# A gated network's exact log decays: step-by-step sums predicted by TensorE prefix sums, one scan of 1.5 elements a step in place of two

## The chip, the cores and the metric

One core of one Trainium2 chip runs the whole program. The metric is the device time of one execution in microseconds; before the change three runs gave 4601.38, 4604.38 and 4605.38 us, median 4604.38.

## The reference

The program is one forward pass over 512 tokens of width 1024: block 1 (a mixer of sparse attention and a gated delta rule, then a mixture of experts) and two layers of block 2. The change lies in block 1's first norm and in the delta rule's log decays:

```python
g = -jnp.exp(a_log) * jax.nn.softplus(a_raw + dt_bias)     # a_raw: columns of h @ w_in, 8 heads
g_cum = jnp.cumsum(g, axis=-1)
decay = jnp.where(causal, jnp.exp(jnp.where(causal, g_cum[..., :, None] - g_cum[..., None, :], 0.0)), 0.0)
```

Here h is the normed input, scaled and shifted by the modulation `silu(c) @ ada_w + ada_b`. Exponentials of differences of sums that reach 1e7 make each rounding of the float32 sums count, so the kernel forms these few sums (16 x 128 columns of the modulation, 512 x 8 entries of a_raw, each of 1024 products) in the order in which the reference adds: one rounding per step.

## The kernel before, in words

The helpers record operations through an object; `mm` is a TensorE matmul, `act` a ScalarE activation, `tt`, `ts`, `stt` and `scan` are VectorE operations, `nc.gpsimd` is GpSimd. A tile framework orders each engine's operations ahead of time by their program order and readiness; on the chip each engine takes its own in that fixed order.

**Modulation (`exact_mod`, lines 737 to 824).** Weights are split into two parts of few bits (wh, wl), as is silu(c) (c1, c2, on diagonals dc), so that every product on TensorE is exact. A unit is 128 output columns (i = 2j + h) and half of the 1024 terms: 32 units. Its 512 leading products go to PSUM and are moved by ScalarE to xq, the middle ones to xms, the small ones to xz. VectorE then makes a first scan (the running sum, as it would be without the small parts), rounds it to the grid by adding and taking off a large M, GpSimd forms two differences, VectorE adds the middle ones, and a second scan of 1024 elements (two a step) rounds the true sum step by step. The second scan of a unit is recorded after the first operations of the next (`late`).

**Decays (`decay_chains`, lines 910 to 1018).** The same for the 512 x 8 entries: 32 units of (half of the terms, pair of heads, block of 128 tokens), eight chains in a row of 1040 elements, a scan of 1040 (az from aq and am), the rounding, the differences and a second scan of 2080 elements. It needs the modulation and each token's rstd. Then come `decay_sums`: a softplus in exact float32 pieces (a long chain of short VectorE operations) and sums over a chunk.

**What lies beside (`front`, drawn by `among` and `spend`, lines 318 to 334).** Each VectorE operation of the exact part adds 0.7 x (0.2 + elements / 960) to a debt, and while the debt is positive the next step of the front is recorded there. The front's steps have costs: keys and values of the memory 2 x 40, small gates 5, compression 32, keys, values, queries and compressed branch 54, attention 8 x 2 x 6.6 = 105.6; together about 277. What is left over is recorded at the end. The front's products use the weight slabs wraw, whi, wlo: 512 KB loaded on SP's queue, split by ScalarE and by VectorE or GpSimd in turn.

Of the eight PSUM banks, two (x) take the exact products, three (g) the gemms, two (t) small products, one (o) outputs.

Of the kernel before, what the change touches and what calls it, by code (L numbers as in the profile page):

```python
# [32 lines left out]
KT = 8  # L33
# [7 lines left out]
# float32 coefficients: exponential, logarithm, log1p (numerator, denominator)  # L41
# [11 lines left out]
# ---------------------------------------------------------------- host layout  # L53
# [41 lines left out]

def _dn_constants():
# [32 lines left out]
def _pack_pv(inp):  # L129
# [13 lines left out]
    add("n1g", _cols(inp["norm1_g"]))  # L143
    add("n2g", _cols(inp["norm2_g"]))
# [19 lines left out]
def pack(inp):  # L164
# [6 lines left out]
    a["ada_w"] = np.ascontiguousarray(inp["ada_w"][0].reshape(KT, 128, 24, 256).transpose(2, 1, 0, 3))  # L171
    w = inp["w_in"][0]
# [5 lines left out]
    a["w1_a"] = _kpn(av)  # L178
# [75 lines left out]
# ---------------------------------------------------------------- the program  # L254
class Net:
# [30 lines left out]
    # ---- small helpers  # L286
# [30 lines left out]
    # the steps of other, a generator of rough costs, among what VectorE does for main  # L317
# [41 lines left out]
    def sub(self, lo, src, hi):  # L359
        """src - hi in SBUF; of every lo_of, lo_pool on GpSimd"""  # L360
# [4 lines left out]
    # ---- weights and products  # L365
# [18 lines left out]
    def rsqrt(self, T, src, n, N=S, out=None):  # L384
        """(src / n + eps) ** -0.5: exponential of the logarithm, then a Newton step"""
# [13 lines left out]
    def sigmoid(self, T, src, shape, tag, bufs=1):  # L399
        """exp(-ln(1 + exp(-z)))"""  # L400
# [7 lines left out]
    def rms64(self, T, out, src, gcol, s, N=S, n=64, op_scale=None):  # L408
        """out = src * g * rsqrt(sum over each half of the partitions / n + eps)"""
# [7 lines left out]
    # ---- column sums of squares over features -> rstd broadcast over partitions  # L417
# [40 lines left out]
    def ada(self, T):  # L458
        """the modulation but for the first shift and scale"""
# [22 lines left out]
    def adaln(self, T, keep):  # L482
        """h = x * rstd * gain + shift"""
# [29 lines left out]
    def near_hi(self, T, a, hi, lo, tag, bits=12):  # L513
        """a rounded to 12 bits, and the rest"""
# [7 lines left out]
    def xprod(self, T, a, b, n):  # L522
        """minus a product, and the product's rounding error"""
# [9 lines left out]
    def xadd(self, T, out, m, e, c, n, big=False):  # L533
        """c - m + e in one rounding; c a tile, a number, or one number for each of equal parts; big: never smaller than m"""
# [3 lines left out]
        def take(o, x, rev=False):  # L538
            """c - x, or x - c"""
# [24 lines left out]
    def xfma(self, T, out, a, b, c, n, big=False):  # L564
        """a * b + c in one rounding"""
# [13 lines left out]
    def xhorner(self, T, y, x, xs, cs, n, big=True):  # L579
        """Horner's rule, each step in one rounding; the first two coefficients on the scalar engine"""  # L580
# [4 lines left out]
    def xexp(self, T, x, n):  # L585
        """exp as (y, 2 ** k)"""
# [15 lines left out]
        # minus the sum of the two parts, and its error  # L602
# [14 lines left out]
    def xdiv(self, T, out, a, b, n):  # L617
        """a / b, rounded once; a a tile or one"""
# [28 lines left out]
    def consts(self, T, rows, n):  # L647
        """[128, steps, parts] of numbers"""
# [6 lines left out]
    def xsoftplus(self, T, out, x, n):  # L655
# [8 lines left out]
        def same(x, k, i):  # L664
            """x, k times, and its parts"""
# [14 lines left out]
        # log1p by a rational function: denominator and numerator  # L680
# [14 lines left out]
        # log(1 + e), 1 <= 1 + e <= 2  # L695
# [22 lines left out]
        # the first below the threshold, the second above  # L718
# [8 lines left out]
    def grid(self, T, out, q, n):  # L727
        """a power of two between 4 and 8 times the largest entry of each row"""
# [8 lines left out]
    def exact_mod(self, X):  # L737
        """the shift and the scale of the first norm: one accumulator per column, one rounding per term"""
        nc = self.nc
        self.mod1 = X.tile([128, 16], F32, name="mod1")  # L740
        with self.pool("xm", side="right") as T:
# [9 lines left out]
            M = T.tile([128, 1], F32, name="xM")  # L751
            st2 = T.tile([128, 2, 2], F32, name="xst")
            def slab(j, half):
                w = T.tile([128, 4, 256], F32, name="xw", bufs=2)
                nc.sync.dma_start(w, self.I["ada_w"][j][:, 4 * half:4 * half + 4, :])
# [3 lines left out]
                self.tt(wl, w, wh, OP.subtract)  # L759
                return wh, wl  # L760

            def products(j, half, h):
                if h == 0:
                    self.xw = slab(j, half)
                wh, wl = self.xw
                cs = slice(128 * h, 128 * h + 128)
                q = T.tile([128, S], F32, name="xq", bufs=2)
                m = T.tile([128, S], F32, name="xms", bufs=2)
                z1 = T.tile([128, 512, 2], F32, name="xz1", bufs=3)
                for out, scale, terms in ((q, 1.0, ((wh, 0),)), (m, 1.0, ((wh, 1), (wl, 0))), (z1[:, :, 0], -1.0, ((wl, 1),))):  # L770
                    p = self.ps("x")
                    for kk in range(4):
                        for n, (a, i) in enumerate(terms):
                            self.mm(p[:, 128 * kk:128 * kk + 128], a[:, kk, cs], dc[:, i, 4 * half + kk, :],
                                    kk == 0 and n == 0, kk == 3 and n == len(terms) - 1)
                    self.act(out, p, scale=scale)
                return q, m, z1

            def sums(j, half, h, q, m, z1):
                st = st2[:, h]  # L780
                z0 = T.tile([128, 513, 2], F32, name="xz0", bufs=2)
                if j == 0 and h == 0 and half == 0:
                    self.grid(T, M, q, "m")
                gh = z0[:, :, 1]
                if half == 0:
                    nc.gpsimd.memset(gh[:, 0:1], 0.0)
                    g0 = d0 = 0.0
                else:
                    g0, d0 = st[:, 0:1], st[:, 1:2]
                    self.act(gh[:, 0:1], g0)  # L790
                self.scan(gh[:, 1:], q, m, g0, op0=OP.add, op1=OP.add)
                self.ts(gh[:, 1:], gh[:, 1:], M, M, OP.add, OP.subtract)
                self.act(z1[:, :, 1], gh[:, 1:])
                t = z0[:, 1:, 0]
                nc.gpsimd.tensor_tensor(t, gh[:, 1:], gh[:, :512], op=OP.subtract)
                nc.gpsimd.tensor_tensor(t, q, t, op=OP.subtract)
                self.tt(t, t, m, OP.add)

                def rest():
                    i = 2 * j + h  # L800
                    d = z1.rearrange("p a b -> p (a b)")
                    self.scan(d, z0[:, 1:].rearrange("p a b -> p (a b)"), d, d0, op0=OP.add, op1=OP.subtract)
                    if half == 0:
                        self.act(st[:, 0:1], gh[:, 512:513])
                        self.act(st[:, 1:2], d[:, 1023:1024])
                    else:
                        self.tt(self.mod1[:, i:i + 1], gh[:, 512:513], d[:, 1023:1024], OP.add)
# [3 lines left out]
            units = [(j, half, h) for j in range(8) for half in range(2) for h in range(2)]  # L811
            ready = products(*units[0])
            late = None
            for n, u in enumerate(units):
                now = ready
                if n < 31:
                    ready = products(*units[n + 1])
                f = sums(*u, *now)
                if late is not None:
                    late()  # L820
                late = f
            late()
            self.tt(self.mod1, self.mod1, self.pv("ada_b", 0, 16), OP.add)
# [1889 lines left out]
```

## Time and profile before

| | |
|---|---|
| median of 3 runs | 4604.38 us (4601.38 to 4605.38) |
| profiled execution, its span | 4600.1 us, 53904 instructions |
| mean granted TensorE clock | 0.900 of full speed |
| PE busy | 3975.4 us (86%) |
| DVE busy | 3086.1 us (67%) |
| ACT busy | 2088.8 us (45%) |
| POOL busy | 1763.2 us (38%) |

PE is TensorE's matmuls, PEld its weight loads, DVE VectorE, ACT ScalarE, POOL GpSimd, SP the queue that issues most loads. All times are in us from the start of the span unless a column says ns. Matmuls are pipelined: the duration of one holds a tail in which the next already runs, so that a busy PE need not be a full one. The granted clock has two levels, 1.0 (2.4 GHz) and 0.5 (1.2 GHz); a mean lies between.

### The profile page before, as it was taken

The numbers are of one execution on the slowest core, as the hardware profiler recorded it, in microseconds if no ns is written. First come the engines' busy times: TensorE is split into PE (matmuls) and PEld (weight loads), VectorE is DVE, ScalarE is ACT, GpSimd is POOL, SyncE is SP. The second block draws the span as 40 slices with busy tenths as digits, with TensorE's granted clock in tenths as the row PEclk, the third lists the DMA queues.
The fourth block names the chain that finished last, engine by engine and source line by source line (L and its number), as shares of the span: only waits on it lengthen the run. The fifth ranks groups of instructions, "written<-read, shape, count | busy, mean of one in ns | idle before, by whom it ended". The sixth has DMA issues, their size and how long they took to land. (4 is left out here: it accounts for less than half of the span.)

```text
span 4600.1 us, 53904 instructions
## 1 busy us (share of the span) xinstructions
PE 3975.4 (86%) x19368; PEld 3192.1 (69%) x19368; DVE 3086.1 (67%) x5074; ACT 2088.8 (45%) x3514; POOL 1763.2 (38%) x1084
## 2 busy tenths in 40 slices
PE   5667757777897888979989999999999898999998
PEld 3566545555776676767867777788877676787886
DVE  8988999998865587857657565433378566665542
ACT  3444546554223276833436544443244365544432
POOL 3445544632321335223326442232234354423431
PEclk9678867777887899989999999999999999999999
DMA  4233201113311588931222242222211132332222
GB/s 141 83 109 111 64 21 46 32 37 118 92 56 36 194 311 318 358 114 57 73 64 88 78 135 83 92 96 91 92 60 64 57 102 66 118 120 74 92 93 82
DMA packets 178958, 473.62 MB, mean 103 GB/s; under 512 B 17176, under 2 KB 32600, under 8 KB 178304
## 3 DMA queue, kind: packets, MB, share of 16 engines
q1 hardware_dynamic: 171872, 445.99, 29.3%
q0 software_dynamic: 6816, 24.15, 1.5%
q8 instruction: 154, 2.52, 0.2%
q14 instruction: 116, 0.95, 0.1%
HBM read 429.66 MB, written 38.29 MB: 102 GB/s over the span
## 5 line engine op out<-in xcount | busy, mean ns | idle before, releaser
L363 POOL TENSOR_TENSOR wlo<-wraw,whi 128x1024 fp32r<-128x1024 f32 (+4 forms) x244 | 566.1, 2320 | 1106.2 <-ACT whi L315 1041.9
L303 PE MATMUL ps_g<-ha,whi 128*128 128x512 f32 x2184 | 896.6, 411 | 63.0 <-DVE mraw L343 22.8
L315 ACT ACTIVATE whi<-wraw 128x1024 fp32r<-128x1024 f32 (+4 forms) x489 | 481.3, 985 | 948.8 <-PE ps_g L303 734.8
L303 PE MATMUL ps_g<-ha,wlo 128*128 128x512 f32 x2184 | 891.5, 408 | 6.3 <-DVE wlo L363 4.2
L303 PE MATMUL ps_g<-hl,whi 128*128 128x512 f32 x2184 | 892.3, 409 | 0.0
L303 PEld LDWEIGHTS ps_g<-ha,whi 128*128 128x128 f32 x2184 | 424.6, 194 | 177.8 <-DVE mraw L343 22.0
L303 PEld LDWEIGHTS ps_g<-ha,wlo 128*128 128x128 f32 x2184 | 424.3, 194 | 108.9 <-DVE wlo L363 4.9
L303 PEld LDWEIGHTS ps_g<-hl,whi 128*128 128x128 f32 x2184 | 424.6, 194 | 102.1 <-issue 3.5
L363 DVE TENSOR_TENSOR wlo<-wraw,whi 128x1024 fp32r<-128x1024 f32 (+4 forms) x245 | 308.5, 1259 | 187.7 <-ACT whi L315 182.2
L339 DVE TENSOR_TENSOR_SCAN az<-az,az 128x2080 f32<-128x2080 f32 x32 | 153.3, 4792 | 4.4 <-POOL az L993 4.2
L303 PE MATMUL ps_g<-fal,whi 128*128 128x512 f32 x352 | 137.0, 389 | 0.0
L303 PE MATMUL ps_g<-fah,whi 128*128 128x512 f32 x352 | 137.0, 389 | 0.0
L303 PE MATMUL ps_g<-fah,wlo 128*128 128x512 f32 x352 | 136.9, 389 | 0.0
L353 DVE SCALAR_TENSOR_TENSOR h_R<-h_R,h_gd,ps_s 128x64 f32<-128x64 f32 x448 | 124.6, 278 | 11.9
L2314 POOL TENSOR_SCALAR mP<-mP,sfst 128x512 f32<-128x512 f32 x64 | 103.0, 1616 | 52.1 <-DVE sfst L2313 25.4
L303 PE MATMUL ps_g<-mlo,xh 128*128 128x512 f32 x272 | 111.8, 411 | 11.4 <-POOL mlo L1913 11.4
L303 PE MATMUL ps_x<-xdc,xwh 128*128 128x128 f32 x256 | 66.7, 350 | 63.1 <-ACT xdc L315 40.6
L1501 POOL TENSOR_TENSOR dnl<-dnn,dnc 128x512 f32<-128x512 f32 x48 | 68.5, 1439 | 137.1 <-DVE dnn L343 70.0
L2528 POOL TENSOR_SCALAR g2z<-g2z 128x512 f32<-128x512 f32 x48 | 81.8, 1705 | 99.8 <-DVE g2z L343 88.8
L988 POOL TENSOR_TENSOR az<-az 128x1024 f32<-128x1024 f32 x32 | 78.7, 2460 | 104.0 <-DVE az L349 69.3
L303 PE MATMUL ps_x<-adw,ahh 128*128 128x256 f32 x256 | 84.1, 392 | 37.8 <-ACT az L315 19.2
L343 DVE TENSOR_TENSOR x<-ps_g,x 128x512 f32<-128x512 f32 x48 | 33.0, 691 | 124.8 <-PE ps_g L303 124.8
(996 smaller groups left out, 10446.2 us busy)
## 6 DMA issues: line engine op xcount, KB each, us to landing
wraw<-w_fm SPq DMA_DIRECT2D x169, 512.0 KB, 3.5
wraw<-f_w SPq DMA_DIRECT2D x120, 512.0 KB, 3.4
mrawa<-moe_g SPq DMA_DIRECT2D x18, 1024.0 KB, 10.6
mrawb<-moe_d SPq DMA_DIRECT2D x18, 1024.0 KB, 6.7
adaw<-ada_w SPq DMA_DIRECT2D x64, 256.0 KB, 2.7
mrawa<-moe_u SPq DMA_DIRECT2D x16, 1024.0 KB, 9.2
mrawb<-moe_u SPq DMA_DIRECT2D x16, 1024.0 KB, 10.4
mrawb<-moe_g SPq DMA_DIRECT2D x14, 1024.0 KB, 10.7
```

The source lines that it names most:

```text
L303: self.nc.tensor.matmul(out, a, b, start=start, stop=stop)
L315: return self.nc.scalar.activation(out, in_, f, **kw)
L339: return self.nc.vector.tensor_tensor_scan(out, *args, **kw)
L343: return self.nc.vector.tensor_tensor(out, a, b, op=op)
L353: return self.nc.vector.scalar_tensor_tensor(out, a, s, b, op0=op0, op1=op1)
L363: e.tensor_tensor(lo, src, hi, op=OP.subtract)
L988: nc.gpsimd.tensor_tensor(t, gh[:, :, 2:], gh[:, :, 1:129], op=OP.subtract)
L1501: nc.gpsimd.tensor_tensor(nl, n_, dnc[:, 1 + lv, None, :].to_broadcast([128, 4, 128]), op=OP.mult)
L2314: nc.gpsimd.tensor_scalar(P, P, st[:, 3:4], None, op0=OP.mult)
L2528: self.nc.gpsimd.tensor_scalar(z, z, ZMIN, None, op0=OP.max)
```

## The change

The first scan, the rounding and the differences' first part are replaced. TensorE multiplies the weights with triangle tables (a prefix sum of the leading and middle products, `tri` scaled by c in `upto`, or by the weights in `times`) and adds M by one more product (`dm` with ones), so that the predicted running sum stands on the grid when it is in PSUM. ScalarE moves it out twice, as the sum and as its negative, into every third element of a row; GpSimd forms the difference d of neighbours; TensorE adds d (by a float32 product with the identity) to all the products and ScalarE moves the sum to the remaining third. One scan with in-row steps of two runs over 1.5 elements a step. The terms are reordered on the host (`_steps`), so that the reference's four accumulators are rows of their own: the modulation goes over all columns of the first half, then the second; the decays have four parts c of two k tiles, 64 units of two heads with both rows of 256 steps in one row of 774 elements. The split wl goes from VectorE to GpSimd, the slab xw has one buffer in place of two. The debt of the front grows by 2.0 with each unit besides what the scan adds, where VectorE's other operations had added theirs.

The parts of the diff that do work on the chip:

```diff
-    def spend(self, out):
+    def spend(self, out, more=0.0):
         if self.other is not None:
-            self.debt += self.ratio * (0.2 + math.prod(out.shape[1:]) / 960)
+            self.debt += more or self.ratio * (0.2 + math.prod(out.shape[1:]) / 960)
...
+            def upto(half):
+                tc = T.tile([128, 2, 1280], F32R, name="xtc")
+                at = 0
+                for kk in range(4):
+                    n = 512 - 128 * kk
+                    for i, c in enumerate((c1, c2)):
+                        self.act(tc[:, i, at:at + n], self.tri[:, :n], scale=c[:, 4 * half + kk:4 * half + kk + 1])
+                    at += n
+                return tc
...
             def slab(j, half):
-                w = T.tile([128, 4, 256], F32, name="xw", bufs=2)
-                nc.sync.dma_start(w, self.I["ada_w"][j][:, 4 * half:4 * half + 4, :])
+                w = T.tile([128, 4, 256], F32, name="xw")
+                nc.sync.dma_start(w, self.I["ada_x"][j][:, 4 * half:4 * half + 4, :])
...
-                self.tt(wl, w, wh, OP.subtract)
+                nc.gpsimd.tensor_tensor(wl, w, wh, op=OP.subtract)
...
+            def path(half, j, h):
...
+                a = T.tile([128, 1538], F32, name="xa", bufs=3)
+                p = self.ps("x")
+                at = 0
+                for kk in range(4):
+                    n = 512 - 128 * kk
+                    for m, (w, e) in enumerate(((wh, 0), (wh, 1), (wl, 0))):
+                        self.mm(p[:, 512 - n:], w[:, kk, cs], tc[:, e, at:at + n], kk == 0 and m == 0, False)
+                    at += n
+                self.mm(p, dm, self.onew, False, True)
...
+                self.act(a[:, 3::3], p, AF.Identity, bias=up)
+                self.act(a[:, 4::3], p, AF.Identity, scale=-1.0, bias=down)
+                d = T.tile([128, S], F32, name="xd", bufs=2)
+                nc.gpsimd.tensor_tensor(d, a[:, 0:1536:3], a[:, 4::3], op=OP.add)
 
                 def rest():
...
+                    p = self.ps("x")
+                    self.mm(p, self.ident, d, True, False)
+                    for kk in range(4):
+                        for n, (w, e) in enumerate(((wh, 0), (wh, 1), (wl, 0), (wl, 1))):
+                            self.mm(p[:, 128 * kk:128 * kk + 128], w[:, kk, cs], dc[:, e, 4 * half + kk, :], False, kk == n == 3)
+                    self.act(a[:, 2::3], p)
+                    self.scan(a[:, 3::2], a[:, 2::2], a[:, 3::2], st[:, i, 1:2] if half else 0.0, op0=OP.add, op1=OP.add)
...
+                    self.spend(None, self.step)
...
+            late = []
+            for u in [(half, j, h) for half in range(2) for j in range(8) for h in range(2)]:
+                late.append(path(*u))
+                if len(late) > 1:
+                    late.pop(0)()
...
+        for c in range(4):
...
             for pr in range(4):
...
+                def times(out, m, e):
+                    n = m.shape[1]
+                    for i in range(2):
+                        nc.gpsimd.tensor_tensor(out[:, i], m[:, None, :].to_broadcast([128, 2, n]),
+                                                wp[:, i, 2 * c + e, hs, None].to_broadcast([128, 2, n]), op=OP.mult)
+
+                times(t0, self.tri[:, :256], 0)
+                times(t1, self.tri[:, :128], 1)
+                for e in range(2):
+                    times(dg[:, e], self.ident, e)
...
+                    for n, (h, i) in enumerate(((hh, 0), (hh, 1), (hl, 0))):
+                        self.mm(p, h[:, 0, tk], t0[:, i].rearrange("p h i -> p (h i)"), n == 0, False)
+                        self.mm(p3[:, :, 128:], h[:, 1, tk], t1[:, i], False, False)
+                    self.mm(p, dm[:, b], self.onew, False, True)
+                    self.act(t[:, :, 7::3], p3, AF.Identity, bias=M[:, b, 1:2])
+                    self.act(t[:, :, 8::3], p3, AF.Identity, scale=-1.0, bias=M[:, b, 0:1])
+                    d = T.tile([128, 2, 256], F32, name="ad", bufs=2)
+                    nc.gpsimd.tensor_tensor(d, t[:, :, 4:772:3], t[:, :, 8::3], op=OP.add)
...
+                        p = self.ps("x")
+                        self.mm(p, self.ident, d.rearrange("p h i -> p (h i)"), True, False)
+                        for e in range(2):
+                            diag(p, tk, e, ((hh, 0), (hh, 1), (hl, 0), (hl, 1)), False, e == 1)
+                        self.act(t[:, :, 6::3], p.rearrange("p (h i) -> p h i", h=2))
+                        f = t.rearrange("p h i -> p (h i)")
+                        self.scan(f[:, 1::2], f[:, 0::2], f[:, 1::2], 0.0, op0=OP.add, op1=OP.add)
+                        nc.gpsimd.tensor_tensor(st[:, c, b, 2 * pr:2 * pr + 2], t[:, :, 772], t[:, :, 773], op=OP.add)
+                        self.spend(None, self.step)
...
+            self.step = 2.0
```

## Rows read from the trace of the kernel before

**Rows 1.** The page's 40 slices: DVE's busy tenths, 115 us each.
```profile
DVE  8988999998865587857657565433378566665542
```
**Rows 2.** Stretches: length, busy us (instructions) of PE, PEld, DVE, ACT, POOL; clock; DMA.
```profile
39.00:1064.00 1025.00, 719.08 (x3302) 570.03 (x3302) 926.20 (x1333) 515.30 (x1061) 497.30 (x328) 0.75 0.22 71
...
996.00:1064.00 68.00, 52.92 (x171) 35.38 (x169) 60.51 (x312) 34.22 (x85) 9.05 (x11) 0.70 0.34 103
...
500.00:550.00 50.00, 44.36 (x224) 37.09 (x225) 41.97 (x26) 25.33 (x48) 31.06 (x19) 0.90 0.23 74
600.00:650.00 50.00, 26.86 (x110) 22.14 (x110) 46.28 (x48) 20.04 (x37) 21.70 (x18) 0.53 0.04 11
1300.00:1350.00 50.00, 44.78 (x348) 37.52 (x346) 40.11 (x91) 15.45 (x29) 15.53 (x11) 0.71 0.14 43
```
**Rows 3.** The stage by tile: az, xz (DVE, ACT, POOL); xwl, ps_x (PE first).
```profile
39.00:1064.00 1025.00, 300.38 (x112) 83.94 (x144) 244.10 (x164) 0.75 0.22 71
39.00:1064.00 1025.00, 180.31 (x144) 47.98 (x112) 117.79 (x78) 0.75 0.22 71
39.00:1064.00 1025.00, 67.89 (x256) 57.08 (x256) 20.91 (x14) 0.75 0.22 71
39.00:1064.00 1025.00, 224.78 (x1024) 187.67 (x1024) 166.04 (x288) 0.75 0.22 71
```
**Rows 4.** DVE groups of the stage, scans: count | busy us, mean ns | idle before, releasers.
```profile
L339 DVE TENSOR_TENSOR_SCAN az<-az,az 128x2080 f32<-128x2080 f32 x32 | 153.3, 4792 | 4.4 <-POOL az L993 4.2
L339 DVE TENSOR_TENSOR_SCAN az<-aq,am 128x1040 f32<-128x1040 f32 x32 | 87.3, 2727 | 5.3 <-ACT am L315 5.0 <-issue 0.3
...
L339 DVE TENSOR_TENSOR_SCAN xz<-xq,xms 128x512 f32<-128x512 f32 x16 | 19.5, 1216 | 11.2 <-ACT xms L315 10.9
```
**Rows 5.** ACT groups of the stage, same columns.
```profile
L315 ACT ACTIVATE az<-ps_x 128x512 f32<-128x512 f32 x64 | 40.5, 634 | 24.6 <-DVE az L339 18.1 <-DVE smst L1124 4.2 <-DVE smst L348 1.4
L315 ACT ACTIVATE aq<-ps_x 128x512 f32<-128x512 f32 x64 | 37.9, 592 | 13.2 <-PE ps_x L303 10.7 <-POOL az L954 1.4 <-POOL wlo L363 0.4
L315 ACT ACTIVATE az<-az 128x1040 f32<-128x1040 f32 x32 | 37.7, 1178 | 24.5 <-DVE az L349 20.5 <-DVE smst L343 2.5 <-DVE smst L348 1.2
...
L315 ACT ACTIVATE xz<-xz 128x512 f32<-128x512 f32 x32 | 21.9, 684 | 60.5 <-DVE xz L349 60.3
...
L315 ACT ACTIVATE rsv<-ps_t,ce 128x512 f32<-128x512 f32 x6 | 4.1, 684 | 1.9 <-DVE rst L343 1.9
```
**Rows 6.** POOL groups of the stage, same columns.
```profile
L363 POOL TENSOR_TENSOR wlo<-wraw,whi 128x1024 fp32r<-128x1024 f32 x33 | 93.1, 2820 | 80.4 <-ACT whi L315 80.4
...
L795 POOL TENSOR_TENSOR xz<-xz 128x512 f32<-128x512 f32 x32 | 55.5, 1733 | 129.9 <-DVE xz L349 114.7 <-DVE mod L343 11.9 <-DVE cact L343 3.2
...
L946 POOL TENSOR_TENSOR adw<-apid,aw 128x1024 fp32r<-128x1024 f32 x16 | 37.1, 2335 | 3.4 <-DVE aw L353 2.7 <-DVE aw L343 0.5 <-PE ps_x L303 0.2
```
**Rows 7.** PE groups of the stage: the front's matmuls of 512 and 256 columns.
```profile
L303 PE MATMUL ps_g<-hl,whi 128*128 128x512 f32 x200 | 87.9, 440 | 0.0
...
L303 PE MATMUL ps_g<-whi,meml 128*128 128x256 f32 x128 | 37.8, 296 | 0.0
```
**Rows 8.** PE in order of time: start us, us, instruction; 128, 256 and 512 columns.
```profile
89.33 0.27 PE L303 MATMUL ps_x<-xdc,xwh 128*128 128x128 f32 x1
89.44 0.27 PE L303 MATMUL ps_x<-xdc,xwl 128*128 128x128 f32 x1
...
104.55 7.07 PE L303 MATMUL ps_g<-fmw,cact 128*1 128x256 f32 x32
...
202.91 0.28 PE L303 MATMUL ps_g<-memh,whi 128*128 128x256 f32 x1
203.03 0.28 PE L303 MATMUL ps_g<-meml,whi 128*128 128x256 f32 x1
...
3000.07 0.39 PE L303 MATMUL ps_g<-ha,whi 128*128 128x512 f32 x1
3000.30 0.39 PE L303 MATMUL ps_g<-hl,whi 128*128 128x512 f32 x1
```

More of the change, by code (lines that the diff above doesn't have):

```diff
@@ L143, in _pack_pv @@
     add("n1g", _cols(inp["norm1_g"]))
+    add("n1gx", _cols(_steps(inp["norm1_g"][0])))
+    add("ada_bx", np.concatenate([_cols(_steps(inp["ada_b"][0, i * D:(i + 1) * D])) for i in range(2)], 1))
     add("n2g", _cols(inp["norm2_g"]))
@@ L171, in pack @@
     a["ada_w"] = np.ascontiguousarray(inp["ada_w"][0].reshape(KT, 128, 24, 256).transpose(2, 1, 0, 3))
+    ax = inp["ada_w"][0][:, :2 * D].T.reshape(2, D, D)
+    ax = np.concatenate([_steps(ax[i]) for i in range(2)]).T
+    a["ada_x"] = np.ascontiguousarray(ax.reshape(KT, 128, 8, 256).transpose(2, 1, 0, 3))
+    p = np.arange(128)
+    a["tri"] = np.concatenate([p[:, None] <= p[None, :], np.ones((128, 384), bool)], 1).astype(np.float32)
     w = inp["w_in"][0]
@@ L766, in products @@
                 cs = slice(128 * h, 128 * h + 128)
[L767 to L770, printed above, removed]
+                if half == i == 0:
                     p = self.ps("x")
                     for kk in range(4):
[L773 to L784, printed above, removed]
+                        self.mm(p[:, 128 * kk:128 * kk + 128], wh[:, kk, cs], dc[:, 0, kk, :], kk == 0, kk == 3)
+                    self.grid(T, M[:, 0:1], p, "m")
+                    self.ts(M[:, 1:2], M[:, 0:1], -1.0)
@@ L785, in sums @@
+                up, down = M[:, 1:2], M[:, 0:1]
                 if half == 0:
[L786 to L794 removed]
@@ L809, in sums @@
-                return rest
[L811 to L823, printed above, removed]
+                    nc.gpsimd.memset(a[:, 0:1], 0.0)
+                else:
+                    self.act(a[:, 0:1], st[:, i, 0:1])
+                    ud = T.tile([128, 2], F32, name="xud", bufs=3)
+                    self.act(ud[:, 0:1], st[:, i, 0:1], AF.Identity, bias=up)
+                    self.act(ud[:, 1:2], st[:, i, 0:1], AF.Identity, scale=-1.0, bias=down)
+                    up, down = ud[:, 0:1], ud[:, 1:2]
@@ L934, in decay_chains @@
-        for half in range(2):
-            hh = T.tile([128, 4, S], F32R, name="ahh", bufs=1)
-            hl = T.tile([128, 4, S], F32R, name="ahl", bufs=1)
-            for kk in range(4):
-                k = 4 * half + kk
-                t = (qs, ms)[kk % 2][kk // 2][:, 0:4, 2:]
-                nc.sync.dma_start(t, self.I["xT"][:, k, :].rearrange("p (c i) -> p c i", c=4))
+        wp = T.tile([128, 2, 8, 8], F32, name="awp")
+        self.near_hi(T, w, wp[:, 0], wp[:, 1], "aw")
+        M = T.tile([128, 4, 2], F32, name="aM")
@@ new lines, in decay_chains @@
+        dm = T.tile([128, 4, 128], F32R, name="adm")
+        st = T.tile([128, 4, 4, 8], F32, name="ast")
+        tiles = [T.tile([128, 2, 774], F32, name="aa%d" % i) for i in range(3)]
+        for t in tiles:
+            nc.gpsimd.memset(t[:, :, 0:6], 0.0)
+            for at, v in ((1, FAR), (2, -FAR)):
+                nc.gpsimd.memset(t[:, :, at:at + 1], v)
+        unit = 0
+        late = []
+        for c in range(4):
+            hh = T.tile([128, 2, S], F32R, name="ahh", bufs=2)
+            hl = T.tile([128, 2, S], F32R, name="ahl", bufs=2)
+            for e in range(2):
+                k = 2 * c + e
+                t = T.tile([128, 4, 128], F32, name="axs", bufs=2)
+                nc.sync.dma_start(t, self.I["xs"][:, k, :].rearrange("p (c i) -> p c i", c=4))
@@ L995, in rest @@
-                    def rest(z0=z0, z1=z1, gh=gh, s=s, half=half):
-                        d = z1.rearrange("p c a b -> p (c a b)")
-                        self.scan(d, z0.rearrange("p c a b -> p (c a b)"), d, 0.0, op0=OP.add, op1=OP.subtract)
-                        if half == 0:
-                            self.act(s[:, 0], gh[:, :, 129])
-                            self.act(s[:, 1], z1[:, :, 129, 1])
-                        else:
-                            nc.gpsimd.tensor_tensor(s[:, 0], gh[:, :, 129], z1[:, :, 129, 1], op=OP.add)
+                    if c == pr == 0:
+                        p = self.ps("x")
+                        for e in range(2):
+                            diag(p, tk, e, ((hh, 0),), e == 0, e == 1)
+                        self.grid(T, M[:, b, 0:1], p, "a")
+                        self.ts(M[:, b, 1:2], M[:, b, 0:1], -1.0)
+                        self.act(dm[:, b], self.ident, scale=M[:, b, 0:1])
@@ L1635, in exact @@
     def exact(self, X):
-        self.exact_mod(X)
-        self.exact_decay(X)
+        nc = self.nc
+        self.mod1 = X.tile([128, 16], F32, name="mod1")
+        self.gct = X.tile([128, 32], F32, name="gct")
+        with self.pool("xk", side="right") as K:
+            self.tri = K.tile([128, S], F32, name="tri")
+            nc.sync.dma_start(self.tri, self.I["tri"])
+            self.onew = K.tile([128, S], F32R, name="onew")
+            self.act(self.onew.rearrange("p (a b) -> p a b", a=4), self.ones[:, None, :].to_broadcast([128, 4, 128]))
+            self.step = 2.0
+            self.exact_mod(K)
+            self.exact_decay(K)
     def front(self, M):
```

119 lines of the change are left out of this document (35 added, 84 removed).

## The prediction

> **What bounds the kernel now.** I read the page's slices first: VectorE (DVE) stands at 8 or 9 tenths through the first eleven slices, some 1260 us, and nowhere after [rows 1]. The code changed runs there, beside the front (keys of the memory, gates, attention), so I next asked for the busy times of the stage from the first product on ps_x (39 us) to the end of the softplus (1064 us): 1025 us, DVE 926 of it (90%), TensorE (PE) 719, ScalarE (ACT) 515, GpSimd (POOL) 497 [rows 2]. The tile sums then say whose work that is: instructions on az, xz and xwl hold DVE for 300 + 180 + 21 = 501 us [rows 3]. So DVE's order of work sets this stage, and over half of it is what the change touches. What follows 1064 us isn't touched and should only move earlier.
>
> **The change, engine by engine.** It keeps the emission order (the front's steps are drawn by a debt), so I sum the work of each engine in the stage, old and new, and then ask what length such loads can pack into.
>
> *DVE.* The 501 us go: both scans, the rounding to the grid, the added products and the split of xw. What comes is 96 scans (32 of 768, 64 of 774 elements). The trace has scans of 512, 1040 and 2080 elements at 1.22, 2.73 and 4.79 us [rows 4]; per element that is 2.3 to 2.6 ns, so a scan of 770 lies between 1.77 and 2.02 us. I take 1.95, as these scans too will share the SBUF with POOL: 187 us. DVE: 926 - 501 + 187 = 612 us. It stops being the bound, by 314 us.
>
> *ACT.* It moves out per new unit three times 512 columns of PSUM, with a step of three elements on the write side. With a step of two it costs 0.63, contiguous 0.59, with a bias column 0.68 [rows 5]. I take 0.66: 96 x 3 x 0.66 = 190 us, and about 25 for tables, diagonals and carried columns. Going: 64 x (0.63 + 2 x 0.59) + 32 x 1.18 of the decay part, 32 x (0.63 + 2 x 0.59 + 0.68) of the other, about 25 of small ones: 258 us. ACT: 515 - 258 + 215 = 472. Were a step of three to cost half as much again, 567; still not the bound.
>
> *POOL.* Going: 244 + 118 us on az and xz [rows 3] and 37 on adw [rows 6]. Coming: 96 sums d of 512 elements, 16 splits of 1024, 16 sets of tables (2560 elements each). A sum of 512 read with a step of two took 1.73, a split 2.82, a table of 1024 elements 2.34 [rows 6]: 96 x 1.73 + 16 x 2.82 + 16 x 5.85 = 305, and some 25 for small ones. POOL: 497 - 399 + 330 = 428.
>
> The new sum d reads both inputs with a step of three floats (12 bytes); no row of before shows such a step on POOL. From the rows, its bounds are 1.17 us (half a table of 1024 elements) and 2.82 us (a whole split of 1024): -54 to +105 us on POOL against 1.73, which I take as the nearest row in size and step.
>
> The Trainium skill (GPSIMD Reference, section 7, Performance pitfalls for Q7 kernels) says that POOL reading SBUF with a step of more than 8 bytes pays about half as much again per element. By that rule d would cost 1.5 x 1.73 = 2.6 us, and POOL would stand at 511 in place of 428. No run shown here has that step.
>
> *PE.* Here the change puts its load. A matmul's duration counts a tail in which the next already runs, so I price by the distance of starts in dense runs at full clock: 128 columns 0.11 us, 256 0.12, 512 0.23, so 384 about 0.18; a plain float32 one of 256 columns 0.22 (32 in 7.07), so one of 512 about 0.44 [rows 8].
> - Before: 512 products of 128 and 512 of 256 columns on ps_x: 56 + 61 = 118 us.
> - A new unit of the modulation: prefix sums 3 x (0.23 + 0.18 + 0.12 + 0.11) = 1.9, the grid's diagonal 0.23, the float32 identity on d 0.44, 16 diagonal products 1.8: 4.35 us, x 32 = 139.
> - A new unit of the decays: 3 x (0.23 + 0.12) + 0.23 + 0.44 + 8 x 0.12 = 2.7 us, x 64 = 170.
> - The rest, unchanged: 600 matmuls of 512 columns (three groups like that shown), 768 of 256 (six groups) [rows 7], 128 of the first fast modulation at 0.22, and some 780 others between 0.11 and 0.23, taken at 0.15: 138 + 92 + 28 + 117 = 375.
> So PE goes from 493 to 684 us at full clock, +191. What this is in time hangs on the granted clock. In stretches of 50 us it was 0.90 where PE was busy for 44 of 50 us, 0.53 where 27, and once 0.71 at 45 [rows 2]. I take 0.90: 760 us. PE becomes the fullest engine.
>
> *How it packs.* PE 760, DVE 612, ACT 472, POOL 428. The chain of a decay unit (prefix on PE 1.3, two moves on ACT 1.3, d on POOL 1.7, products on PE 1.4, a move on ACT 0.7, scan on DVE 1.95) is some 8 us, but the next unit's prefix lies between d's start and the products. With one bank of ps_x for the prefixes and one for the products, a unit alone needs PE's own time and some 0.7 us of waits: 32 x 5.05 + 64 x 3.4 = 379 us, so the chain isn't the limit while front work fills the gaps. Two things are late next. The first is that engines of like load wait for each other in their fixed orders: I give PE's 760 us a tenth, 76. The second is the softplus, a chain of short DVE operations: it took 68 us with the last of the front beside it [rows 2]. The debt now grows by 2.0 and 0.7 x (0.2 + 770 / 960) = 0.7 a unit, 2.7; with the small operations (some 37) the modulation brings it to about 124, so the front's 277 cost units are used up after some 56 of the 64 decay units, and the chain runs uncovered; PE had 53 busy us there. I charge 44. Stage: 760 + 76 + 44 = 880 us in place of 1025, that is -145.
>
> A check from the other side: now 719 + 926 + 515 + 497 = 2657 busy us in 1025, 2.59 engines at once. With the new loads (PE in the same measure 719 - 225 [rows 3] + 309 / 0.9 = 837) it is 2349, at 2.59 again 907 us: -118. I stay with -145, because the fixed DVE order is no longer in the way.
>
> The loads added before the stage are small: two tables of 256 KB on SP's queue (512 KB loads land in under 5 us) and the slab xw with one buffer in place of two, which is reloaded once in two units (near 10 us): nothing.
>
> **Sum.** The profiled execution spans 4600.1 us, 4.3 below the median of the runs, 4604.4. 4600.1 - 145 + 4.3 = 4459, rounded to 4460.
>
> **Rivals.**
> 1. *TensorE stays at the clock it has* (the other side). The mean granted clock of the stage is 0.75 [rows 2]. If the many short groups leave it there, PE needs 684 / 0.75 = 912, and with the 120 us of waits 1032: +7 us, 4611. At 0.70 it is 977 + 120 = 1097: +72, 4676. From 0.755 down the change loses. For it: the 45-of-50 stretch at 0.71; the new work has many products of 128 and 256 columns with hand-overs between. Against: low clocks stand in stretches where PE idles for DVE, and that idling is what goes.
> 2. *POOL's sum d ends last.* If d takes as long as a split of 1024, 2.82 us [rows 6], 1.09 more in 96 units are 105 us; half to all of it on the path leaves -92 to -40: 4512 to 4564, in the middle 4538. For it: d sits between two PE steps, and POOL's queue also has splits of 2.8 us and tables. Against: POOL is at 428 of 880 us. By the Trainium skill's rule on steps (GPSIMD Reference, section 7, Performance pitfalls for Q7 kernels) d would cost the 2.6 us worked out above, and with all of the 83 us on the path the time would be 4543.
> 3. *PE packs densely.* At a clock of 1.0 and 5% waits, 684 / 0.95 + 40 = 760: -265, 4339. For it: later stretches of the kernel hold PE at 9 tenths; against: there it isn't fed by three engines in turn.
> 4. *The DVE saving isn't there*: strided scans cost more than the rows, say 3 us. Then DVE is 713, still under PE; no change in the forecast. It has no share of its own.
>
> **How the numbers follow.** The forecast (4380 to 4535) gets 0.64, rival 3 with all below 4380 0.14, rival 2 and other small gains (4535 to 4595) 0.12, rival 1 0.10, of which 0.03 falls within 0.2% and 0.07 slower. About 0.2% (9 us) is what a measurement of this kernel can tell from no change. Faster: 0.64 + 0.14 + 0.12 = 0.90. The range, 4335 to 4560, reaches over rival 3's price and most of rival 2's, and leaves out about 0.05 below and 0.14 above; it also holds the ends of d and of the scans.
>
> **What would show it.** Right: the end of the softplus near 920 us in place of 1064; DVE near 612 busy us before it, PE the fullest engine at a granted clock near 0.9; scans of 770 elements near 1.95 us, d near 1.73, moves by ACT near 0.66; front tiles ending before the last decay units. The step on PE is wrong if the clock stays near 0.75 or the spacing of the prefix products is far from 0.12 to 0.23; the step on POOL if d takes over 2.2 us and PE's waits are for d. The forecast as a whole fails if the stage is longer than 1016 us, or if a stage after it changes its own length by more than 20 us.

## The result: 4466 us, and the profile after

The changed kernel takes 4466.08 us (median of 4 runs, 4463.02 to 4469.62), beside 4603.18 for the kernel before on the same chip: a ratio of 0.9705 (95% interval 0.9691 to 0.9719), some 136 us less. The forecast was 4460.

The page's slices of the changed kernel (40 of 112 us): PE's busy tenths, DVE's, and the granted clock.
```profile
PE   5998899858879789799899999999999899999998
...
DVE  5658766678745778677656655332577475665542
...
PEclk9998999978878899899999999999999899999999
```
DVE's wall of 8s and 9s [rows 1] is gone from the first slices, and from the second to the eighth PE stands at 8 or 9 instead. The stretches of the changed kernel (length; busy us and instructions of PE, PEld, DVE, ACT, POOL; clock; DMA share; GB/s): the modulation's units, the preparation of the decays, their units, the softplus, and the whole stage.
```profile
39.00:375.00 336.00, 318.47 (x2062) 270.79 (x2063) 190.40 (x247) 186.79 (x330) 133.21 (x79) 0.97 0.39 131
375.00:411.00 36.00, 24.57 (x104) 19.04 (x103) 31.08 (x109) 14.42 (x28) 15.36 (x20) 0.76 0.29 98
411.00:886.00 475.00, 443.22 (x2207) 338.80 (x2206) 320.89 (x607) 336.57 (x602) 262.23 (x272) 0.96 0.14 48
886.00:928.00 42.00, 0.00 (x0) 0.00 (x0) 37.90 (x219) 2.31 (x11) 2.13 (x17) 0.50 0.23 76
...
39.00:928.00 889.00, 786.26 (x4370) 628.62 (x4370) 580.25 (x1181) 540.09 (x970) 412.93 (x385) 0.93 0.25 83
```
The stage took 1025 us [rows 2] and takes 889, -136: it holds the whole gain, and all that follows only moved earlier. PE is now 88% busy (70% before), DVE 65% (90% before). Two things are not as one would draw them: the modulation's own stretch is no shorter (it ended at 348 us before, at 375 now, with PE at 95%), and beside the softplus PE does nothing at all.

The new operations of the stage, by group (count | busy us, mean ns | idle before, releasers): scans, moves by ScalarE, then GpSimd's sums d, tables, and the split of weights.
```profile
L352 DVE TENSOR_TENSOR_SCAN aa<-aa 128x774 f32<-128x774 f32 x64 | 126.9, 1982 | 62.2 <-ACT aa L328 61.7
...
L352 DVE TENSOR_TENSOR_SCAN xa<-xa 128x768 f32<-128x768 f32 x16 | 37.6, 2350 | 53.5 <-ACT xa L328 53.5
```
```profile
L328 ACT ACTIVATE aa<-ps_x,aM 128x512 f32<-128x512 f32 x128 | 111.9, 952 | 32.2 <-PE ps_x L316 21.2 <-POOL ast L1015 9.6 <-PE ps_o L316 1.1
...
L328 ACT ACTIVATE aa<-ps_x 128x512 f32<-128x512 f32 x64 | 55.3, 865 | 32.1 <-PE ps_x L316 31.7
```
```profile
L1005 POOL TENSOR_TENSOR ad<-aa 128x512 f32<-128x512 f32 x64 | 86.6, 1353 | 40.1 <-ACT aa L328 39.5
L376 POOL TENSOR_TENSOR wlo<-wraw,whi 128x1024 fp32r<-128x1024 f32 x33 | 81.3, 2464 | 97.6 <-ACT whi L328 96.7 <-DMA wraw<-x_wv 0.5 <-issue 0.4
L972 POOL TENSOR_TENSOR adg<-cst,awp 128x256 fp32r<-128x256 f32 x64 | 58.0, 937 | 21.3 <-PE ps_x L316 21.3
L972 POOL TENSOR_TENSOR at<-tri,awp 128x512 fp32r<-128x512 f32 x32 | 50.5, 1597 | 27.2 <-PE ps_x L316 26.7 <-DVE awp L366 0.5
...
L972 POOL TENSOR_TENSOR at<-tri,awp 128x256 fp32r<-128x256 f32 x32 | 27.7, 883 | 0.0
```
And one decay unit's products in order of time, at full clock (start us, us): the float32 product that adds d (two records), then eight diagonal products.
```profile
438.96 1.02 PE L316 MATMUL ps_x<-ad,cst 128*128 128x512 f32 x2
439.42 0.80 PE L316 MATMUL ps_x<-adg,ahh 128*128 128x256 f32 x2
440.05 0.40 PE L316 MATMUL ps_x<-adg,ahl 128*128 128x256 f32 x2
440.29 0.40 PE L316 MATMUL ps_x<-adg,ahh 128*128 128x256 f32 x2
```
From 438.96 to 440.05 is 1.09 us for that product and two diagonal ones of 0.12: it holds PE for some 0.85 us, twice the forecast's 0.44.

### The profile page after: what moved, and what is told of

The parts are those of the page before. It is cut to its first block, busy times and chain, and to the rows that moved or that the text cites. A ratio compares the mean times of both kernels' runs of the same rounds, so it can differ in the third digit from the quotient of the medians.

```text
span 4461.4 us, 56050 instructions
## 1 busy us (share of the span) xinstructions
PE 4041.6 (91%) x20436; PEld 3251.8 (73%) x20436; DVE 2737.4 (61%) x4912; ACT 2113.8 (47%) x3424; POOL 1684.9 (38%) x1144
## 5 line engine op out<-in xcount | busy, mean ns | idle before, releaser
L376 POOL TENSOR_TENSOR wlo<-wraw,whi 128x1024 fp32r<-128x1024 f32 (+4 forms) x244 | 554.6, 2273 | 1119.9 <-ACT whi L328 1060.3
L376 DVE TENSOR_TENSOR wlo<-wraw,whi 128x1024 fp32r<-128x1024 f32 (+4 forms) x245 | 294.7, 1203 | 204.6 <-ACT whi L328 198.5
L352 DVE TENSOR_TENSOR_SCAN aa<-aa 128x774 f32<-128x774 f32 x64 | 126.9, 1982 | 62.2 <-ACT aa L328 61.7
L328 ACT ACTIVATE aa<-ps_x,aM 128x512 f32<-128x512 f32 x128 | 111.9, 952 | 32.2 <-PE ps_x L316 21.2
L328 ACT ACTIVATE mhi<-mrawa 128x2048 fp32r<-128x2048 f32 x52 | 99.6, 1915 | 32.0 <-PE ps_g L316 11.9
L328 ACT ACTIVATE g2z<-g2z 128x512 f32<-128x512 f32 x144 | 90.3, 627 | 49.6 <-POOL g2z L2548 48.1
L356 DVE TENSOR_TENSOR mlo<-mrawb,mhi 128x2048 fp32r<-128x2048 f32 x42 | 102.7, 2470 | 17.8 <-ACT mhi L328 17.8
```

Source lines behind the costliest of these rows:

```text
L328: return self.nc.scalar.activation(out, in_, f, **kw)
L352: return self.nc.vector.tensor_tensor_scan(out, *args, **kw)
L356: return self.nc.vector.tensor_tensor(out, a, b, op=op)
L376: e.tensor_tensor(lo, src, hi, op=OP.subtract)
```

## The experiments

Theory A: TensorE's work sets the new stage, so that only PE time removed, or PE's idle time filled, helps. Rivals: ScalarE's slow moves and the hand-overs of a unit (C), GpSimd's order (D). The us given below are differences of the ratios times 4603; each comparison is with the kernel before, on the same chip.

**Each part alone.** `old_mod` puts the old modulation code beside the new decays, `old_decay` the reverse.
```diff
-                    self.scan(a[:, 3::2], a[:, 2::2], a[:, 3::2], st[:, i, 1:2] if half else 0.0, op0=OP.add, op1=OP.add)
...
+                self.scan(gh[:, 1:], q, m, g0, op0=OP.add, op1=OP.add)
...
+                    self.scan(d, z0[:, 1:].rearrange("p a b -> p (a b)"), d, d0, op0=OP.add, op1=OP.subtract)
```

> The modulation's sums as before (two scans a unit), the decays' as changed. In the trace the changed modulation ends 27 us later than the old one (375 in place of 348 us) and the decays' units took 475 in place of 625 us. Theory A, each part's share is what its own stretch shows: the change of the modulation is worth nothing or loses, so with the old one the time is 4440 to 4475. Theory B, the change of each part pays by the VectorE time that it saves (some 139 of 314 us are the modulation's) and the stretches only trade front work between them: the old modulation costs 139 / 314 of 138, about 60 us, so about 4525.

> The complement: the modulation's sums as changed, the decays' as before (the changed constants for the permuted order are left out where they have no use). Theory A (the share is what the stretches show): no gain from the modulation, 4595 to 4630. Theory B (shares by the VectorE time saved): 60 us gained, about 4543.

Measured: 4500.71 us, ratio 0.978 (0.9763 to 0.9796), and 4593.19 us, 0.9982 (0.9972 to 0.9991). So the decays alone bring 101 us, the modulation alone 8, both 136. Neither of these two expectations' theories (A, shares by stretch; B, shares by VectorE time saved) holds for both orders: the modulation's part is worth 8 us while the old decays stand behind it, and 35 beside the new ones. The stage of the two, `old_mod` first, and for `old_decay` also its part up to the end of the modulation:
```profile
39.00:971.00 932.00, 744.61 (x3886) 597.45 (x3886) 694.28 (x1281) 522.02 (x970) 443.21 (x404) 0.89 0.24 78
```
```profile
39.00:1058.00 1019.00, 758.18 (x3786) 596.56 (x3786) 802.43 (x1232) 533.34 (x1062) 449.52 (x309) 0.80 0.22 72
...
39.00:373.00 334.00, 316.74 (x2043) 269.48 (x2044) 186.76 (x258) 185.66 (x327) 132.14 (x78) 0.96 0.40 129
```
The new modulation took 124 us off DVE (926 to 802) and moved the end of the stage by 6: behind it DVE is busy for 802 - 187 = 616 of 685 us (90%), so with the old decays the stage still hangs on DVE there. A stretch's length (375 in place of 348 us) isn't its part's share either, since front work is dealt to both.

**TensorE loaded and unloaded.** `pe_heavy` adds two products with zeros in each unit; `pe_light` makes the product that adds d a one-pass one (d is rounded for it, so the kernel leaves out its lower bits).
```diff
+                for _ in range(2):
+                    self.mm(p, dm, self.zw, False, False)
                 self.mm(p, dm, self.onew, False, True)
```
```diff
-                    self.mm(p, self.ident, d, True, False)
+                    self.mm(p, self.idr, d, True, False)
```


> Each of the 96 units issues two more products of 512 columns, with a table of zeros, among its prefix sums: 2 x 0.23 us of TensorE, 44 us in all at full clock, 46 at 0.96. Theory A, TensorE's own time sets the stage: +40 to +50 us, about 4511. Theory B, TensorE has slack in its hand-overs (its starts account for only some 671 of 889 us) and ScalarE's slow moves (0.95 us) or the sum d end last: +0 to +15, up to 4481.

> The sum d is written in the rounded float32 type and the identity table is of that type too, so that the product that adds d is one pass; d loses its lower bits, so the decay sums are no longer the exact ones. In the trace of the changed kernel the plain float32 product of 512 columns takes some 0.9 us from its start to the next free slot at full clock, not the 0.44 of the prediction's sum; the one pass takes 0.23. So 96 x 0.67 = 64 us of TensorE go. Theory A, TensorE's time counts at the half that the added products showed (24 of 44 us in the profile): -25 to -40, about 4434. Theory B, TensorE sets the stage in full: -64, about 4402. Theory C, ScalarE's moves and hand-overs set it, and TensorE's load only lengthens their chain when it grows: 0 to -10.

Measured: 4485.7 us, 0.9743 (0.9727 to 0.976), +17 for 44 us added; 4437.1 us, 0.9644 (0.9628 to 0.966), -28 for about 60 removed (0.85 - 0.23 in 96 units). The stages, `pe_heavy` first:
```profile
39.00:952.00 913.00, 820.47 (x4562) 655.82 (x4562) 579.05 (x1182) 545.73 (x971) 396.44 (x385) 0.95 0.25 81
```
```profile
39.00:904.00 865.00, 748.83 (x4274) 622.84 (x4274) 588.39 (x1182) 536.18 (x970) 412.99 (x385) 0.92 0.26 85
```
A microsecond of PE is worth about 0.4 of stage when added and 0.5 when removed (by the intervals, each give or take 0.2). In the profiles PE's busy time rose by 34 us and the stage by 24, then fell by 37 and 24: part of the change is taken from PE's idle time or added to it (103 us in the changed kernel, 93 and 116 here). So TensorE matters, yet not alone. Both edits also lengthen or shorten every unit's chain of hand-overs by the same time, and these two runs don't tell TensorE's load from that chain.

**PE's idle time beside the softplus.** `step150` deals less front work to each unit.
```diff
-            self.step = 2.0
+            self.step = 1.5
```

> The front work drawn by each unit is cut from 2.0 to 1.5 cost units, so that some 21 of the front's 277 units stand beside the softplus, where TensorE idles for 47 us now. Theory A, TensorE sets the stage: 21/277 of the front's TensorE time (375 / 0.96 = 390 us) leaves the busy part, -30, and the softplus grows by 10 to 15 us for the VectorE work between its steps: -15 to -20, about 4448. Theory B, the units' own chain sets the stage and front work fits in for nothing: the units' part stays and the softplus grows: +10 to +15, about 4478.

Measured: 4454.61 us, 0.9681 (0.9665 to 0.9697): -11, on A's side but short of its 15 to 20; its interval still overlaps that of the change (0.9691 to 0.9719). The last stretch of its trace shows the front at work there:
```profile
881.00:923.00 42.00, 25.55 (x80) 16.08 (x80) 40.61 (x196) 19.44 (x49) 8.97 (x11) 0.68 0.48 151
```

**Moves and banks.** `dve_move` gives each unit's third move to VectorE (first edit, here that of the modulation), `x3` deals the banks anew (second edit).
```diff
-                    self.act(a[:, 2::3], p)
+                    nc.vector.tensor_copy(a[:, 2::3], p)
```
```diff
-                    with self.banks({"x": 2, "g": 3, "t": 2, "o": 1}, {"s": "g"}) as self.PS, pool("XR", side="right") as XR:
+                    with self.banks({"x": 3, "g": 2, "t": 2, "o": 1}, {"s": "g"}) as self.PS, pool("XR", side="right") as XR:
```

> The third move of each unit (PSUM to every third element, 0.86 us on ScalarE) is done by VectorE: ScalarE -82 us of 540, VectorE +96 x 0.6 to 0.9 = +58 to +86 of 580. Theory A, TensorE sets the stage: -5 to +10. Theory C, ScalarE's moves (0.95 and 0.86 us in place of the 0.66 predicted) end last in the hand-overs: -20 to -40. A third outcome, VectorE's own order binds: +20 to +60.

> Three PSUM banks for the units' products and two for the front's, in place of two and three. If the units' products wait for their banks (a prefix sum can't start before the two moves of the unit before it have emptied the bank), -10 to -25. If TensorE's own load sets the stage, -3 to +3 from the units, and up to +15 where the front's products wait for their two banks.

Measured: 4460.51 us, 0.9686 (0.967 to 0.9702), and 4455.56 us, 0.9677 (0.9661 to 0.9693). Here too both intervals overlap that of the change: -9 and -13 (each give or take some 10) are likely gains but not shown ones. ScalarE lost 66 us of work (540 to 474) for some 9, so its load is not what the stage mainly waits for. The move itself stayed as long (0.85 us on VectorE, 0.86 on ScalarE), so whether its length in a unit's chain counts is not shown.

**The units without the front.** `serial` draws no front work until the units and the softplus are through.
```diff
-            self.step = 2.0
+            self.step = -1e-6
...
-                        self.among(self.front(M), 0.7, lambda: self.exact(X))
+                        self.among(self.front(M), 0.0, lambda: self.exact(X))
```

> No front work is drawn while the units run: all of it (277 cost units) comes after the softplus. The units then show their own length. The prediction's 32 x 5.05 + 64 x 3.4 = 379 us, with 0.46 us more for the float32 product in each (44 us): 423 us if TensorE's own time and 0.7 us of hand-overs set a unit; with ScalarE's moves as measured a unit's chain from the prefix sum over two moves (1.9 us) and d (1.35 us) is 3.3 us, which the next prefix and the products (1.3 + 2.1 us) just cover, so no more than 10% above that. If the chain isn't covered, a decay unit takes prefix, moves, d, products and move one after the other over two units, 8 us / 2 = 4 us or more, and the units take over 450 us. The whole time is then that of the changed kernel plus 60 to 130 us.

Measured: 4725.27 us in the one timed run. In the trace the units begin at 44 us, end at 629, and the softplus at 673. The decays' units, and then the front by itself (it ends near 1200):
```profile
316.00:629.00 313.00, 249.41 (x1078) 180.14 (x1077) 143.60 (x92) 164.60 (x193) 229.56 (x238) 0.86 0.01 2
...
673.00:1194.00 521.00, 429.89 (x2027) 334.78 (x2027) 214.18 (x593) 246.95 (x494) 83.01 (x46) 0.84 0.30 97
```
A decay unit alone takes some 5.1 us (301 to 629 us for 64), where 3.4 + 0.4 was worked out. PE's own work in one is 2.7 + 0.4 = 3.1 us at full clock, 3.6 at the 0.86 granted here, which leaves about 1.5 us of waits: the hand-overs are not covered by the next prefix. What PE waits for there, and what POOL waits for (total us, times, longest):
```profile
PE ps_x L316 <- POOL ad L1005: 61.9, 23, 4.0
...
POOL ast L1015 <- DVE aa L352: 38.4, 21, 3.4
```
One such wait in order of time (start us, us, in brackets the idle time before): four tables, the sum of two numbers (ast), d, and then PE.
```profile
449.65 6.10 POOL L972 TENSOR_TENSOR at<-tri,awp 128x512 fp32r<-128x512 f32 x4
...
455.72 0.19 POOL L1015 TENSOR_TENSOR ast<-aa 128x2 f32<-128x2 f32 x1
455.87 1.29 POOL L1005 TENSOR_TENSOR ad<-aa 128x512 f32<-128x512 f32 x1
...
457.21 2.08 PE L316 MATMUL ps_x<-ad,cst 128*128 128x512 f32 x2 [3.84 <-POOL ad L1005]
```
By this run's means POOL's queue holds 9.5 us of tables (2 x 1.60 + 2 x 1.19 + 4 x 0.99) for every four units, and the sum ast, which stands for the scan ahead of the next d. The price for the whole run (+60 to +130) was wrong, it came to some +260: the front alone took 521 us with PE at 83% and no other engine over half, so it too has waits of its own. One after the other the two take 634 + 527 us, laid into each other 889, so the overlap is worth some 270.

**GpSimd's queue, and d in two parts.** `tab_dve` builds the diagonal tables on VectorE; `dsplit` cuts d so that two one-pass products add it.
```diff
-                    times(dg[:, e], self.ident, e)
+                    times(dg[:, e], self.ident, e, nc.vector)
```
```diff
+                    self.act(dh[:, 0], d)
+                    nc.vector.tensor_tensor(dh[:, 1], d, dh[:, 0], op=OP.subtract)
...
-                        self.mm(p, self.ident, d.rearrange("p h i -> p (h i)"), True, False)
+                        for k in range(2):
+                            self.mm(p, self.idr, dh[:, k], k == 0, False)
```


> The diagonal tables of the decays (64 operations of 256 elements at 0.94 us on GpSimd) are built by VectorE: GpSimd -60 us of 413, VectorE some +25 to +40 of 580. With the units alone, GpSimd's queue (sums d behind 9 us of tables, and carried pairs that wait for the scan) held TensorE up by 62 us. Theory D, that queue also costs time beside the front: -8 to -20. Theory A, TensorE's time decides, since it waits only some 11 us for d there: -5 to +5.

> The sum d is cut into two parts of the rounded float32 type (upper part by ScalarE 0.6 us, rest by VectorE 0.6 us, ahead of the next unit's prefix sums), and added by two one-pass products of 0.23 us in place of one plain float32 product of 0.9: TensorE -42 us, ScalarE and VectorE each +58. Nothing of the sums is lost. Theory A, a TensorE microsecond is worth 0.45 to 0.55 of stage: -15 to -25. Theory C, ScalarE (540 + 58 of 889 us) and the longer chain of a unit decide: +5 to +30.

Measured: 4445.19 us, 0.9666 (0.965 to 0.9682): -18, in D's range, with an interval clear of the change's own. And 4515.39 us, 0.9816 (0.9799 to 0.9832): +51, past even C's 30. The stages, `tab_dve` first:
```profile
39.00:912.00 873.00, 779.46 (x4370) 623.16 (x4369) 594.58 (x1247) 540.56 (x969) 354.98 (x321) 0.95 0.25 84
```
```profile
39.00:979.00 940.00, 795.67 (x4370) 657.12 (x4369) 646.00 (x1279) 590.32 (x1065) 443.74 (x385) 0.89 0.23 78
```
PE's waits for d in the decays, in the changed kernel (411 to 881 us) and in `tab_dve` (411 to 866 us):
```profile
PE ps_x L316 <- POOL ad L1005: 8.2, 6, 2.9
```
```profile
PE ps_x L316 <- POOL ad L1005: 4.9, 3, 2.7
```
They fell by 3 us only. So the tables on GpSimd cost time, but how the rest of the 18 us comes about isn't shown.

In `dsplit`, two waits in the decays (430 to 900 us):
```profile
DVE adh L1021 <- ACT adh L328: 48.3, 20, 5.4
...
POOL ad L1017 <- DVE adh L1021: 22.5, 11, 5.2
```
No engine is fuller than 85%, but d now passes POOL, ACT and DVE before PE may go on; PE's clock fell to 0.89. The edit also gives the decays' d one buffer in place of two, so that the next d waits until the last one is split (second line); the two causes aren't separated. Together they cost more here than some 40 us of PE work give back. Of A that leaves this, as far as one run shows: PE's time is gained only where no hand-over is added for it.

**The gains together.** `combo1` is `step150` and `x3`; `all4` adds `tab_dve`, and moves the sum ast to VectorE.
```diff
-                        nc.gpsimd.tensor_tensor(st[:, c, b, 2 * pr:2 * pr + 2], t[:, :, 772], t[:, :, 773], op=OP.add)
+                        nc.vector.tensor_tensor(st[:, c, b, 2 * pr:2 * pr + 2], t[:, :, 772], t[:, :, 773], op=OP.add)
```

> Two of the edits that gained together: 1.5 cost units of front work a unit, and three banks for the units' products. If their gains stand apart (front work beside the softplus; banks of the units): -11.5 - 10.5 = -22, about 4444. If both fill the same idle TensorE time: -10 to -14, about 4454.

> The edits that gained, together: 1.5 cost units a unit, three banks for the units' products, the decays' diagonal tables on VectorE; and one new: the sum of a unit's carried pair (two numbers, 0.19 us) is done by VectorE behind its scan, so that GpSimd's queue no longer stands for the scan (87 us of waits in the changed kernel, 129 with the tables on VectorE). If the gains add up without the new edit: -20 - 19.5 = about -40, 4427. Theory D, GpSimd's order is a limit of its own: 5 to 20 us more, 4407 to 4422. Theory E, all these edits fill the same idle TensorE time: no more than -28, over 4438.

Measured: 4446.28 us, 0.9663 (0.9647 to 0.968), -19, and 4449.14 us, 0.9667 (0.9654 to 0.968), -17. The first two edits nearly add up; the other two add nothing to them (theory E). `tab_dve`, `dsplit`, `combo1` and `all4` are read as timings alone: that their sums are still the exact ones is not shown. The stage of `all4` up to the front's last tiles, and those tiles by name (min/median/max ns, first and last start):
```profile
39.00:915.00 876.00, 802.81 (x4371) 633.24 (x4371) 624.07 (x1313) 548.28 (x971) 356.74 (x257) 0.95 0.26 83
```
```profile
L356 DVE TENSOR_TENSOR ya<-ps_o,P x8: 674/683/684, 669.8 to 914.3; 64x512 f32<-64x512 f32 x8
```
Its units end at 806 us in place of 881 and its softplus at 879, but the front then runs on to 914: the units got 75 us shorter, in part because 48 of the front's 277 cost units were left for later, and those now end last. PE is busy for 803 of 876 us. Across the runs that keep PE's work (the change 786, `tab_dve` 779, `all4` 803), the stage is that sum and 73 to 103 us of idle time, and the edits fill the same idle time. Whether a step nearer 2.0 with these edits would go lower wasn't tried.

## Why the prediction was right

The time was right to 6 us. The mechanism was right too (DVE's work goes, and PE with its hand-overs sets the new stage), but that the sum came so close is in part luck: several of its terms were off and cancelled.

- *DVE stops being the bound.* Right: 612 forecast, 580 measured, by two misses. Decay scans of 774 took 1.98 us against 1.95, but those of 768 in the modulation 2.35 to 2.51, above the upper bound of 2.02: 205 us of scans in place of 187. The work that the change doesn't touch fell from 425 to 375 us, which the sum had left as it was. About half of that lies in one group, whose code is the same: 64 additions of one number a row, with a median of 0.16 and 0.17 us, took 47 us before and 23 after, so that most of their mean is something else than the addition, most likely waiting.
```profile
L343 DVE TENSOR_TENSOR smst<-smst,smt 128x1 f32<-128x1 f32 x64 | 47.1, 748 | 0.8
```
```profile
L356 DVE TENSOR_TENSOR smst<-smst,smt 128x1 f32<-128x1 f32 x64 | 22.8, 358 | 1.8
```
- *PE becomes the fullest engine at a better clock.* Right: clock 0.93 over the stage against 0.75 [rows 2], which falsifies rival 1. That PE's idling for DVE had kept the clock down is in line with this.
- *PE's load, 684 at full clock, 760 as run.* An estimate from the trace adds up each record's time to the next start, capped at the dense spacing of its form. It gives 700 to 730 at full clock and 727 to 760 as run, by which spacing is called dense. One miss inside: the float32 product of 512 columns costs 0.85, not 0.44, so some 40 us more in the units (about 350, not 309). The row was misread: `fast_mod` issues 64 float32 products of 256 columns (8 groups of columns, 8 products each), and the trace has 128 records of them, two for each, as for the product that adds d. So the 32 records in 7.07 us [rows 8] are 16 products of 0.44, and twice that is 0.88.
```profile
L303 PE MATMUL ps_g<-fmw,cact 128*1 128x256 f32 x128 | 33.4, 425 | 0.0
```
  The clock, 0.93 over the stage and 0.96 to 0.97 beside the units in place of 0.90, took most of that back.
- *Waits, 76.* By the same estimate 889 - 47 = 842 less 727 to 760 leaves 82 to 115, so the term was too low. `serial` shows the step in it that failed: "a unit alone needs PE's own time and some 0.7 us of waits". A decay unit alone takes 5.1 us, not 3.4: 0.4 more for the float32 product, 0.5 for the clock of 0.86, and waits of about 1.5 in place of 0.7. That the front work covers most of these waits and not all is argued from the 82 to 115 us, not shown.
- *Softplus, 44 uncovered.* PE is idle for 47 us there; right in size. But the front's work ran out later than worked out: its last tile comes with the last decay unit (880 us), not eight units earlier.
- *ACT, 472.* Wrong, 540: the moves took 0.95 and 0.86, not 0.66. It was forecast not to matter up to 567; `dve_move` is in line with that for ScalarE's load.
- *POOL, 428, d 1.73.* 413 measured, by misses that cancelled: d took 135 us in place of 166 (1.35 in the decays, 1.51 in the modulation), the splits of xw 36 for 45 and those of wlo 81 for 93, the tables 136 for 94. The row that d was priced from is a mean as well: its 1.73 stands for durations from 1.04 to 4.16 us with a median of 1.35.
```profile
L795 POOL TENSOR_TENSOR xz<-xz x32: 1038/1350/4158, 48.3 to 341.5; 128x512 f32<-128x512 f32 x32
```
```profile
L1005 POOL TENSOR_TENSOR ad<-aa x64: 1288/1317/2762, 425.7 to 877.5; 128x512 f32<-128x512 f32 x64
```
(Here min/median/max ns and first and last start.) The Trainium skill (GPSIMD Engine Reference, section 7, Performance pitfalls for Q7 kernels) would have a step of 12 bytes cost half as much again, by the estimate in the prediction 2.6 us. The trace doesn't agree: a quarter more at best (1.29 in place of 1.04), none in the median (1.32 and 1.35); that form of rival 2 falls. What was right in rival 2 is the place: GpSimd's queue does hold units up, through its tables (`tab_dve`, -18; the wait shown for `serial`). Whether a shorter d would gain time was not tried.

So 760 + 76 + 44 came out as 727 to 760, 115 to 82, and 47.

## What to carry to other kernels

Here an engine at 90% was relieved, and the stage fell to the next fullest one plus the hand-overs; the waits of a unit were the term underrated, so measure a unit by itself before pricing them. A mean duration can be far above the median (0.75 and 0.16 us here): look at the least and the median before carrying it over to a kernel in which other engines are less busy, and count a row's records against the products in the code. Gains that each filled the idle time of the new bound did not add up. Work spread by a hand-set debt must be dealt anew once the units it is spread over get shorter, or the saving turns up as a tail, as in `all4`.

## What the hardware showed that was not expected

- A ScalarE move of 512 columns out of PSUM that writes every third float took 0.86 us as a copy and 0.95 with a bias column, where a step of two took 0.63 and none 0.59 [rows 5]; VectorE's copy of the same shape took 0.85. GpSimd's sum that reads every third float took 1.29 at best and 1.32 in the median (64 in the decays), where one with a step of two took 1.04 at best, 1.35 in the median and 1.73 in the mean before [rows 6].
- A plain float32 product of 512 columns held PE for 0.85 us and shows as two records, one of 256 columns for 0.44, in two as well; the one-pass product of 512 takes 0.23.
